# Group softmax: shorter programs, first tile loaded row by row, and stores that stand one row sooner

## The chip, the cores and the metric

The kernel runs on one core of a Trainium2 chip. The metric is device time in microseconds (us) of one execution. A *span* is the profiled execution; the time of the same run is 1.8 us longer. In the views DVE is VectorE, ACT is ScalarE and SP is SyncE; a q behind the name (ACTq, SPq) stands for the instruction queue of that engine, and L102 is a line of the kernel.

## The reference

```python
B, N, D, G = 4, 4096, 4352, 8                 # x: float32
x_g = x.reshape(B, N, G, D // G)              # 8 groups of 544 in a row
exp = np.exp(x_g - x_g.max(axis=-1, keepdims=True))
out = exp / exp.sum(axis=-1, keepdims=True)
```

There are 16,384 rows. 285 MB are read and 285 MB written. A tile is two rows on each of 128 partitions, so there are 64 tiles; "row n" below is row n of a partition, 0 to 127.

## The kernel before

SyncE issues the loads, into six tile buffers. VectorE takes each row's eight maxima and later scales the row. ScalarE does the exps with their sums, and issues the stores. A load waits until the store that used its buffer six tiles earlier is complete.

```python
def vector_max(n):
    s = n % S
    if s % R == 0:
        take(nc.vector, landed[s // R], 16)
        nc.vector.sem_inc(seen, 1)
    nc.vector.reduce_max(out=mx[:, s, :], in_=row(s), axis=X, negate=True).then_inc(max_done, 1)
...
def scalar_tile(j, *targets):                 # LAG = 2: tile j's exps, tile j-2's store
    take(nc.scalar, seen)
    for r in range(R):
        if r < len(targets):
            store((j - LAG + r) % NT, targets[r])
        scalar_exp(j * R + r)
...
for t in range(nt):                           # SyncE
    b = t % NT
    if t >= NT:
        nc.sync.wait_ge(stored[b], 16 * (t // NT))
    nc.sync.dma_start(out=bufs[b][:, :], in_=xt[t]).then_inc(landed[b], 16)
...
for j in range(LAG):                          # ScalarE
    scalar_tile(j)
with loop(nc.scalar) as u:                    # loop head placed at slot 0 of a fetch block
    for b in range(NT):
        scalar_tile(LAG + b, turn_out[u, b])
scalar_tile(nt - 2, ot[nt - 4])
scalar_tile(nt - 1, ot[nt - 3], ot[nt - 2])
store((nt - 1) % NT, ot[nt - 1])
...
def vector_rows(lo, hi):                      # VectorE
    for n in range(lo, hi):
        vector_max(n + 1)
        vector_scale(n)
```

## Time and profile before

| | before |
|---|---|
| time, median of 4 runs | 1329.49 us (1329.46 to 1329.67) |
| span of the profile | 1327.6 us |
| VectorE / ScalarE busy | 1206.9 us (91%) / 764.3 us (58%) |
| DMA | 570.48 MB, mean 430 GB/s |

The page's list of DMA issues gives the median time from issue to landing:

```profile
xt<-in_x_dram SPq DMA_DIRECT2D x64, 4352.0 KB, 29.2
out_dram<-xt ACTq DMA_DIRECT2D x64, 4352.0 KB, 51.2
```

A tile takes 20.57 us of DMA for its load and its store, so about 1.4 loads and 2.5 stores stand in the queues at any time.

### The profile page before, as it was taken

How to read it: one execution, taken by the hardware profiler on the slowest of the kernel's cores; microseconds unless marked ns; L12 is line 12 of the kernel's file. 1: busy time of each engine (PE TensorE's matmuls, PEld its weight loads, DVE VectorE, ACT ScalarE, POOL GpSimd, SP SyncE). 2: the span in 40 equal slices, each digit the busy share in tenths (PEclk: the TensorE clock that was granted, in tenths of full speed). 3: DMA queues.
4: the chain of work that ended last, by engine and by line, in shares of the span. 5: the costliest groups of instructions: out<-in, count | busy, mean ns of one | idle time of the engine just before them, and what ended most of it. 6: DMA issues, size and time to landing. Idle time of an engine off the chain costs nothing. (4 is left out here: it accounts for less than half of the span.)

```text
span 1327.6 us, 3432 instructions
## 1 busy us (share of the span) xinstructions
DVE 1206.9 (91%) x384; ACT 764.3 (58%) x2049; POOL 0.2 (0%) x4
## 2 busy tenths in 40 slices
DVE  5999999999999989899898898988989889898892
ACT  3565656565656655565565655655556555565551
POOL 0000000000000000000000000000000000000000
DMA  9999999999999999999999999999999999999997
GB/s 403 418 436 436 434 431 429 435 435 435 434 426 433 436 435 433 431 430 434 436 435 434 425 434 436 435 433 431 429 435 436 434 434 428 432 435 436 433 430 335
DMA packets 18438, 570.48 MB, mean 430 GB/s; under 512 B 2048, under 2 KB 2048, under 8 KB 2048
## 3 DMA queue, kind: packets, MB, share of 16 engines
q1 hardware_dynamic: 9216, 285.22, 49.8%
q10 hardware_dynamic: 9216, 285.22, 49.7%
q14 instruction: 6, 0.05, 0.0%
HBM read 285.21 MB, written 285.21 MB: 430 GB/s over the span
## 5 line engine op out<-in xcount | busy, mean ns | idle before, releaser
L90 ACT ACTIVATE xt<-xt,mx 128x544 f32<-128x544 f32 x1024 | 751.2, 734 | 534.9 <-ACTq L59 534.9
L70 DVE TENSOR_REDUCE mx<-xt 128x8 f32<-128x4352 f32 x128 | 599.0, 4681 | 76.7 <-DVEq L59 75.2
L78 DVE TENSOR_TENSOR xt<-xt,rs 128x4352 f32<-128x4352 f32 x128 | 600.6, 4692 | 18.8
L90 ACT ACTIVATION_READ_ACCUMULATOR xt<-xt,mx 128x1 f32 x1024 | 191.0, 187 | 0.0
L75 DVE RECIPROCAL rs<-sm 128x8 f32<-128x8 f32 x128 | 24.7, 193 | 2.9 <-DVEq L59 2.9
L122 ACT ACT_TABLE_LOAD x1 | 1.3, 1283 | 0.9 <-SPq L47 0.9
L158 POOL MEMSET const-bfloat16-1.0<- 128x1 bf16 x1 | 0.1, 102 | 0.0
L158 POOL MEMSET const-uint8-127<- 128x1 uint8 x1 | 0.1, 102 | 0.0
L158 POOL MEMSET const-float32-0.0<- 128x1 f32 x1 | 0.1, 100 | 0.2 <-issue 0.2
L158 POOL MEMSET const-float32-1.0<- 128x1 f32 x1 | 0.1, 99 | 0.0
## 6 DMA issues: line engine op xcount, KB each, us to landing
xt<-in_x_dram SPq DMA_DIRECT2D x64, 4352.0 KB, 29.2
out_dram<-xt ACTq DMA_DIRECT2D x64, 4352.0 KB, 51.2
```

Source lines behind the costliest of these rows:

```text
L70: nc.vector.reduce_max(out=mx[:, s, :], in_=row(s), axis=X, negate=True).then_inc(max_done, 1)
L75: nc.vector.reciprocal(out=rs[:, s, :], in_=sm[:, s, :]).then_inc(rec_done, 1)
L78: nc.vector.tensor_tensor(out=xr, in0=xr, in1=rs[:, s, :].unsqueeze(2).to_broadcast([P, G, Dg]), op=mybir.AluOpType.mult,).then_inc(scaled, 1)
L90: i = nc.scalar.activation(out=xr[:, g, :], in_=xr[:, g, :], func=Exp, bias=mx[:, s, g:g + 1], scale=1.0, accum_out=sm[:, s, g:g + 1],)
L122: nc.scalar.preload_act_table(Exp)
L158: nc = _bacc.Bacc("TRN2", target_bir_lowering=False, num_devices=1)
```

## The change

It makes the programs shorter, no longer places the loops at the head of a fetch block (a block is the piece in which an engine's program is fetched), and starts the compute sooner by loading the first tile row by row. It also moves the stores: tile t's store now stands behind the exp of row 2t+2, where before it stood behind that of row 2t+3. At the end, row 125 is scaled ahead of row 126's max, and the store of tile 62 stands ahead of the exp of row 126 instead of behind it.

```diff
-    with loop(nc.scalar) as u:                       # placed at a fetch block
-        for b in range(NT):
-            scalar_tile(LAG + b, turn_out[u, b])
...
+    for r in range(R):                               # first tile, row by row
+        nc.sync.dma_start(out=bufs[0][:, r * D:(r + 1) * D], in_=x0[:, r, :]).then_inc(
+            first[r - 1] if r else landed[0], 16)
...
+    scalar_exp(0)
+    with nc.scalar.Fori(0, turns) as u:
+        for t in range(NT):
+            for n in range(t * R + 1, t * R + R + 1):
+                scalar_exp(n)
+            store(t, turn_out[u, t])
+    for n in range(turns * S + 1, nr):
+        if n == (nt - 1) * R:
+            store(nt - 2, dram(of, nt - 2))
+        scalar_exp(n)
+        if n % R == 0 and n < (nt - 1) * R:
+            store(n // R - 1, dram(of, n // R - 1))
+    store(nt - 1, dram(of, nt - 1))
...
+    vector_rows(lead + turns * S, (nt - 1) * R - 1)
+    vector_scale((nt - 1) * R - 1)                   # row 125 scaled first
+    vector_max((nt - 1) * R)
+    vector_rows((nt - 1) * R, nr - 1)
+    vector_scale(nr - 1)
```

More of the change, by code (lines that the diff above doesn't have):

```diff
@@ L6 @@
 from concourse._compat import with_exitstack
-from concourse.ordered_engine_set import OrderedEngineSet
 @with_exitstack
@@ L22 @@
     S = R * NT
-    LAG = 2
     xf = x.flatten_outer_dims()
@@ L27 @@
     Dg = D // G
-    nt = N // (P * R)
-    turns = (nt - LAG) // NT
-    rest = LAG + turns * NT
-    assert rest == nt - 2
+    nr = N // P
+    nt = -(-nr // R)
+    last_rows = nr - (nt - 1) * R
+    turns = (nt - 2) // NT
     f32 = mybir.dt.float32
@@ L34, with dram @@
     Exp = mybir.ActivationFunctionType.Exp
-    xt = xf.rearrange("(t p r) d -> t p (r d)", p=P, r=R)
-    ot = of.rearrange("(t p r) d -> t p (r d)", p=P, r=R)
-    turn_out = of[:turns * S * P, :].rearrange("(u b p r) d -> u b p (r d)", b=NT, p=P, r=R)
+    def dram(af, t):
+        lo, r = P * R * t, R if t < nt - 1 else last_rows
+        return af[lo:lo + P * r, :].rearrange("(p r) d -> p (r d)", p=P)
+    turn_out = of[:turns * P * S, :].rearrange("(u b p r) d -> u b p (r d)", b=NT, p=P, r=R)
     landed = [tc.alloc_semaphore(f"landed{b}") for b in range(NT)]
+    first = [tc.alloc_semaphore(f"first{r}") for r in range(1, R)]
     stored = [tc.alloc_semaphore(f"stored{b}") for b in range(NT)]
-    seen = tc.alloc_semaphore("seen")
     max_done = tc.alloc_semaphore("max_done")
@@ L51, with tile_of @@
     rs = ctx.enter_context(nc.sbuf_tensor("rs", [P, S, G], f32))
-    def loop(engine):
-        return nc.Fori(
-            0, turns, engines=OrderedEngineSet([engine.engine]), head_slot={engine.engine: 0})
     def take(engine, sem, n=1):
         engine.sem_inc(sem, -n).wait_op(sem, n, "sem-ge")
+    def tile_of(t):
+        return bufs[t % NT][:, :(R if t < nt - 1 else last_rows) * D]
     def row(s):
@@ L68, in vector_max @@
             take(nc.vector, landed[s // R], 16)
-            nc.vector.sem_inc(seen, 1)
+        elif n < R:
+            take(nc.vector, first[n - 1], 16)
         nc.vector.reduce_max(out=mx[:, s, :], in_=row(s), axis=X, negate=True).then_inc(max_done, 1)
@@ L98, in scalar_exp, with store @@
         i.then_inc(exp_done, 1)
-    def store(b, target):
-        take(nc.scalar, scaled, R)
-        nc.scalar.dma_start(out=target, in_=bufs[b][:, :]).then_inc(stored[b], 16)
-    def scalar_tile(j, *targets):
-        take(nc.scalar, seen)
-        for r in range(R):
-            if r < len(targets):
-                store((j - LAG + r) % NT, targets[r])
-            scalar_exp(j * R + r)
-    for t in range(nt):
-        b = t % NT
+    def store(t, target):
+        take(nc.scalar, scaled, R if t < nt - 1 else last_rows)
+        nc.scalar.dma_start(out=target, in_=tile_of(t)).then_inc(stored[t % NT], 16)
+    x0 = xf[:P * R, :].rearrange("(p r) d -> p r d", r=R)
+    for r in range(R):
+        nc.sync.dma_start(out=bufs[0][:, r * D:(r + 1) * D], in_=x0[:, r, :]).then_inc(
+            first[r - 1] if r else landed[0], 16)
+    for t in range(1, nt):
         if t >= NT:
-            nc.sync.wait_ge(stored[b], 16 * (t // NT))
-        nc.sync.dma_start(out=bufs[b][:, :], in_=xt[t]).then_inc(landed[b], 16)
+            nc.sync.wait_ge(stored[t % NT], 16 * (t // NT))
+        nc.sync.dma_start(out=tile_of(t), in_=dram(xf, t)).then_inc(landed[t % NT], 16)
     for t in range(nt - NT, nt):
@@ L122 @@
     nc.scalar.preload_act_table(Exp)
-    for j in range(LAG):
-        scalar_tile(j)
-    with loop(nc.scalar) as u:
-        for b in range(NT):
-            scalar_tile(LAG + b, turn_out[u, b])
-    scalar_tile(nt - 2, ot[nt - 4])
-    scalar_tile(nt - 1, ot[nt - 3], ot[nt - 2])
-    store((nt - 1) % NT, ot[nt - 1])
+    scalar_exp(0)
[11 more added lines that the diff above has]
+    store(nt - 1, dram(of, nt - 1))
     def vector_rows(lo, hi):
@@ L136, in vector_rows @@
             vector_scale(n)
+    lead = R - 1
     vector_max(0)
-    vector_rows(0, LAG * R)
-    with loop(nc.vector):
-        vector_rows(LAG * R, LAG * R + S)
-    vector_rows(rest * R, nt * R - 1)
-    vector_scale(nt * R - 1)
+    vector_rows(0, lead)
+    with nc.vector.Fori(0, turns):
+        vector_rows(lead, lead + S)
+    vector_rows(lead + turns * S, (nt - 1) * R - 1)
[3 more added lines that the diff above has]
+    vector_scale(nr - 1)
 _INS = ['x']
```

## The prediction

> **What bounds the kernel now.** I read the page's slices first, then its groups, then the DMA queue's waits, then the timeline and the windows of the two edges.
>
> ```profile
> DMA  9999999999999999999999999999999999999997
> DMA packets 18438, 570.48 MB, mean 430 GB/s; under 512 B 2048, under 2 KB 2048, under 8 KB 2048
> q14 instruction: 6, 0.05, 0.0%
> L90 ACT ACTIVATE xt<-xt,mx 128x544 f32<-128x544 f32 x1024 | 751.2, 734 | 534.9 <-ACTq L59 534.9
> L70 DVE TENSOR_REDUCE mx<-xt 128x8 f32<-128x4352 f32 x128 | 599.0, 4681 | 76.7 <-DVEq L59 75.2
> L78 DVE TENSOR_TENSOR xt<-xt,rs 128x4352 f32<-128x4352 f32 x128 | 600.6, 4692 | 18.8
> ```
>
> The DMA engines are full in every slice but the last. A row costs VectorE 4.68 + 4.69 + 0.19 = 9.55 us, a tile of two rows 19.1 us; a tile costs ScalarE 2 x 5.97 us (eight activations; the timeline's first row runs 18.94 to 24.91). The trace's packet records give the transfers: a tile is 8 packets of 34,816 B on each of 16 DMA engines, 1.288 us each and 1.285 us from start to start, so 10.285 us for a load or a store alone. Load and store of a tile take 20.57 us of DMA against 19.1 of VectorE: DMA is the bound, VectorE has 7% to spare. Each transfer also leaves 16 packets of 4 B, one an engine, by which I can time each engine.
>
> Sixty-four tiles are 1024 packets an engine: 1024 x 1.285 = 1315.8 us, starting at 1.96. Most engines end at 1319.8 to 1320.4, which leaves about 2 us for slow packets at the start and at the first store. Three end later, at 1321.2, 1322.4 and 1325.55. The last one slips by 0.094 us in every tile (its 4-byte packet of the loads is 5.2 us behind the median by load 63): it alone sets the end.
>
> ```profile
> 1309.00:1319.00 10.00, 0.00 (x0) 0.00 (x0) 0.00 (x0) 1.00 1.01 435
> 1319.00:1322.00 3.00, 0.00 (x0) 0.00 (x0) 0.00 (x0) 1.00 0.22 93
> 1322.00:1325.60 3.60, 0.00 (x0) 0.00 (x0) 0.00 (x0) 1.00 0.05 19
> ```
>
> In these windows (the last two columns are DMA share and GB/s) all compute is over and one engine drains alone. So only two things can move the time: how long that last engine is busy, and whether it ever runs dry.
>
> **What the Trainium skill says.** (1) "DMA: Bandwidth & Descriptors", Queues, rings and completion order: a DMA engine goes round-robin between the queues that have work. The trace agrees: with loads and stores both queued a tile takes 20.57 us, alone 10.29. (2) The same page, Latency and other measured facts: engines 7 and 15 are usually slower, with a guessed cause. Here one engine is, by 0.094 us a tile; the records I have do not number it. (3) "Runtime: NRT & Kernel Launch", Instruction fetch mechanics: each sequencer fetches its program by its own DMA queue in blocks of 16 KiB (256 instructions), and a taken branch outside the window stalls for a fetch. The trace agrees on the queue and the stall, not on the size: its fetches are 8192 B, so 128 slots of 64 B. They lie at 47.8, 53.7, 58.3, 64.5, 118.1 and 1267.8 us. ScalarE branches to its loop at 46.0 and goes on at 49.5, 1.3 us after the first fetch.
>
> **The change part by part.**
>
> *Fewer fetches.* Each fetch takes one DMA engine 0.31 us and lengthens its next packet by 0.24 to 0.54 us, so the six cost about 4 us of DMA engine time. The fetch at 1267.83 starts where the 4-byte packet of the engine that ends at 1322.4 ends (1267.82 to 1267.83): the ones I can place are not on the last engine. Worth: 0 on the path.
>
> *The first tile by rows.* 34,816 B take 1.288 us and 8,192 B 0.309, so 17,408 B about 0.648 (estimate): no DMA time is added. Row 0 lands 8 x 0.645 = 5.16 us sooner, at 8.4 instead of 13.55. VectorE starts 0.58 later as before, at 9.0. DMA stays full from 1.96 either way, so by itself this is worth 0.
>
> *The first store comes much earlier.* Before:
>
> ```profile
> 49.86 5.48 ACTq L102 DMA_DIRECT2D out_dram<-xt  x1
> ```
>
> Stores lag two tiles, and the first issue is stuck for 5.48 us; it ends 1.37 us after the fetch at 53.66, and every later store takes 0.34 us, so I read it as a wait for that fetch. Its first packet starts at 56.67. After: max of row 0 ends 13.6, exp 13.8 to 19.7, second exp to 25.7; VectorE scales row 0 from 20.2 to 24.9, takes row 2's max to 29.5, scales row 1 to 34.5; exp of row 2 runs to 35.6. The store stands behind that exp and issues with its last activation, at 35.2, with no fetch near. Adding 0.34 + 1.33: first packet at 36.9.
>
> *What that does to the balance.* From the first store on, each engine moves one load packet for one store packet while both queues hold some. So the number of tiles landed and not yet stored, call it A, freezes at what was loaded before stores began. Before, loads had six tiles in by 71.9 and ran dry until 80.85 while stores went on: A = 6 - 1.49 = 4.51. It is still 4.51 at load 63 (landed at 1273.7 by the median engine, with 59.49 stores done). After: two tiles had landed plus one at 33.75, and 36.9 is 0.31 tile further, so **A = 3.31**. The load queue then keeps 2.7 tiles and never runs dry; store 1 (issue 54.5) just meets the end of store 0 (58.6), later ones gain 1.5 us a tile.
>
> *The tail.* When the last load lands, A tiles of stores remain.
>
> ```profile
> 1279.82 4.69 DVE L70 TENSOR_REDUCE mx<-xt 128x8 f32<-128x4352 f32 x1 [1.48 <-DVEq L59]
> 1284.76 4.69 DVE L78 TENSOR_TENSOR xt<-xt,rs 128x4352 f32<-128x4352 f32 x1
> 1300.62 4.69 DVE L78 TENSOR_TENSOR xt<-xt,rs 128x4352 f32<-128x4352 f32 x1
> 1305.42 0.34 ACTq L102 DMA_DIRECT2D out_dram<-xt  x1
> ```
>
> Before: it lands on the slow engine at 1279.11, the last store issues at 1305.42, 26.3 us later, first packet about 1307.1; that engine has other stores until 1315.27, so it never idles (8 us to spare). After: the last landing moves to 1325.55 - 3.31 x 10.285 = 1291.5. The order of the last tile also changes: row 125 is scaled ahead of row 126's max. From the landing: exp of 125 ends at 0.4, its scale 0.9 to 5.6, max 126 to 10.2, exp 126 to 16.3, exp 127 to 22.3, scale 127 to 27.5, issue 27.6. The queue holds 2.31 tiles beside the last one, 23.8 us, so it runs dry for some 5 us. The last store issues at 1319.1; load 0 at an empty start took 12.6 us from issue to landing (0.95 to 13.55): 1331.7. Add 2.0 us to the span's end and 1.9 from span to time, both as before: **1335.6**.
>
> **The rivals.** (a) The first store is stuck for 5.5 us after all, since it is the first DMA of that queue. For it: only that one issue was slow. Against: SyncE's first took 0.38 us, and the fetch ends 1.37 us before. A would be 3.31 + 5.5/10.285 = 3.84, the queue lasts 29.2 us beside the last store, first packet of which is needed at 29.2: nothing lost, 1329.5. (b) Fetches do load the last engine, and the tail does not bite: four or five fewer, 0.7 us each, 1326. Against: the placed one is elsewhere, and the slip is even over the run. (c) VectorE becomes the bound by a later start: it has 7% to spare and starts 5 us sooner, so no. (d) A store queue that runs dry early (a fetch on ScalarE near slot 128 of its program): loads gain, A rises by up to 0.25, 1333.
>
> **Range and chances.** I give the tail about 0.7, (d) partly mixed into it, (a) 0.2, (b) 0.1. I shade the point to 1335.0. The range 1328.0 to 1338.0 takes in (a) and (d) and leaves 2.4 us for a longer tail. Two per cent is 26.6 us, which nothing here reaches: faster 0.01, same 0.98, slower 0.01.
>
> **What would show it.** First store issue near 35 us and short; at the last load's landing about 3.3 tiles of stores left rather than 4.5; DMA share falling well below full for several us between 1310 and 1320, then full again for the last store; the last issue near 1319; one or two fetches during the run. I am wrong if DMA stays full to 1320 (then A was higher, or the last tile quicker), or if the late engine is no longer late.

## The result, and the profile after

The changed kernel took **1332.38 us** (median of 4, 1332.17 to 1332.48), against 1329.49 before: 2.9 us longer. The ratio is 1.0021, with a 95% interval of 1.0004 to 1.0039. By the 2% rule that is the same. A ratio here is the mean time of one kernel's runs over that of the other's runs of the same rounds, so it is not quite the ratio of the medians.

The page after, in the rows that answer to those of before:

```profile
DMA  9999999999999999999999999999999999999996
q14 instruction: 4, 0.03, 0.0%
L70 DVE TENSOR_REDUCE mx<-xt 128x8 f32<-128x4352 f32 x128 | 599.1, 4681 | 85.8 <-DVEq L55 85.8
out_dram<-xt ACTq DMA_DIRECT2D x64, 4352.0 KB, 39.0
xt<-in_x_dram SPq DMA_DIRECT2D x63, 4352.0 KB, 54.2
```

The work of an instruction is unchanged, and two fetches of six are gone. What changed is the last two rows. Loads now stand 54.2 us in their queue and stores 39.0, where before it was 29.2 and 51.2. The queue has turned from stores to loads, and when the loads are over there is less left to do.

The timeline after, first store and last tile (start, duration, what):

```profile
34.54 0.40 ACTq L102 DMA_DIRECT2D out_dram<-xt  x1
...
1291.12 4.69 DVE L78 TENSOR_TENSOR xt<-xt,rs 128x4352 f32<-128x4352 f32 x1
1295.73 9.27 DVE L70 TENSOR_REDUCE mx<-xt 128x8 f32<-128x4352 f32 x2
1306.99 4.69 DVE L78 TENSOR_TENSOR xt<-xt,rs 128x4352 f32<-128x4352 f32 x1
1312.84 4.69 DVE L78 TENSOR_TENSOR xt<-xt,rs 128x4352 f32<-128x4352 f32 x1
1317.63 0.34 ACTq L102 DMA_DIRECT2D out_dram<-xt  x1
```

The first store issues at 34.5 and is not held up; before, it issued at 49.9 and was held up for 5.48 us. The last load lands at 1290.4 (before 1279.1), and the last store issues at 1317.6 (before 1305.4). The windows at the end of the changed kernel show what DMA did in between (the stretch, its length, busy time of VectorE, ScalarE and GpSimd, PEclk, which is 1.00 throughout, and then DMA share and GB/s):

```profile
1301.00:1311.00 10.00, 8.22 (x3) 10.00 (x29) 0.00 (x0) 1.00 0.82 355
1311.00:1316.00 5.00, 4.04 (x3) 1.34 (x4) 0.00 (x0) 1.00 0.05 21
1316.00:1321.00 5.00, 1.53 (x1) 0.00 (x0) 0.00 (x0) 1.00 0.52 223
1321.00:1326.00 5.00, 0.00 (x0) 0.00 (x0) 0.00 (x0) 1.00 1.04 446
1326.00:1331.00 5.00, 0.00 (x0) 0.00 (x0) 0.00 (x0) 1.00 0.52 223
```

Between 1311 and 1316 DMA stands almost still while VectorE and ScalarE finish the last tile, and then it runs full for the last store alone. The trace also keeps a record of every DMA packet, with its queue, start, duration and size, but not the number of its DMA engine. By these records, the median DMA engine ends the store of tile 62 at 1309.9 and the slowest at 1314.9; the last store's first packets start at 1318.5. The slowest engine was dry (without work) for 3.6 us, the median one for 8.6.

### The profile page after: what moved, and what is told of

Read it like the earlier page. It is cut to its first block, busy times and chain, and to the rows that moved or that the text cites. A ratio compares the mean times of both kernels' runs of the same rounds, so it can differ in the third digit from the quotient of the medians.

```text
span 1330.7 us, 3304 instructions
## 1 busy us (share of the span) xinstructions
DVE 1208.2 (91%) x384; ACT 764.2 (57%) x2049; POOL 0.2 (0%) x4
## 6 DMA issues: line engine op xcount, KB each, us to landing
xt<-in_x_dram SPq DMA_DIRECT2D x63, 4352.0 KB, 54.2
xt<-in_x_dram SPq DMA_DIRECT2D x2, 2176.0 KB, 10.1
```

## The experiments

The theory in one line: the number of tiles landed but not yet stored, A, freezes when stores begin. At the last landing, A tiles of stores remain, of which all but the last must cover the compute of the last tile. I read A from each trace at the landing of tile 62 (loads landed less stores done, by the median DMA engine, a store in progress counted by its share of the time between two landings): 4.51 before, 3.375 after. A is not quite frozen everywhere: with the first tile by rows in the kernel before it goes from 4.63 at tile 40 to 4.50, and without placed loops there from 4.57 at tile 10 to 4.30.

How long the slowest engine is dry can be worked out from A: the time from the last landing to the first packet of the last store, less (A - 1) x 10.285 us of other stores. In the changed kernel the first is 27.3 us to the issue and 0.85 from there to the packets (1317.63 to 1318.48), so 28.1 - 24.4 = 3.7 us dry, and 3.6 was measured. Four buffers (A = 2.75) give 10.1, measured 10.1; the end order of before (26.2 us to the issue) gives 2.6, measured 2.5; A = 3.875 leaves nothing dry, and none was seen.

Ten kernels were made, and one of them was run twice. They were run at other times. Times are medians. The kernel before, in the same calls, took 1329.58, 1329.46 and 1329.60 us. The changed kernel was not run again in them; with five buffers, where A is the same, it took 1332.26 us there. Against the kernel before, every one of them is the same by the 2% rule; differences of 1 to 9 us from the changed kernel are read here only where the ranges do not overlap, unless the text says so.

| kernel | A | expected | us (range) |
|---|---|---|---|
| changed | 3.375 | | 1332.38 (1332.17 to 1332.48) |
| changed, first tile whole | 3.875 | 1329.3 | 1329.23 (1328.87 to 1329.31) |
| changed, stores a tile later | 4.50 | 1329.3 | 1327.62 (1327.53 to 1329.12) |
| the same again | | 1327.6 or 1329.3 | 1327.75 (1327.54 to 1332.17) |
| changed, end order of before | 3.375 | 1331.4 | 1331.37 (1330.97 to 1331.52) |
| changed, four buffers | 2.75 | 1339.4 | 1340.97 (1339.68 to 1341.73) |
| changed, five buffers | 3.375 | 1332.4 | 1332.26 (1332.22 to 1332.56) |
| changed, last tile stored by rows | 3.375 | 1328.7 | 1328.79 (1328.50 to 1328.90) |
| changed, loops at fetch blocks | 3.59 | 1332.4 | 1331.99 (1329.22 to 1339.19) |
| before, loops not at fetch blocks | 4.30 | 1329.5 | 1329.47 (1328.73 to 1332.96) |
| before, first tile by rows | 4.50 | 1329.5 | 1329.80 (1327.90 to 1329.98) |
| before, a load on 15 engines | | 1326 to 1331 | 1337.34 (1335.81 to 1339.44) |

One correction to texts: where they give the first packet of the first store (36.15 in the changed kernel, 56.67 before), I had taken the first lengthened *load* packets for it. By queue, its first packets start at 39.6 and 60.1.

### First tile loaded whole

```diff
-    for r in range(R):
-        nc.sync.dma_start(out=bufs[0][:, r * D:(r + 1) * D], in_=x0[:, r, :]).then_inc(
-            first[r - 1] if r else landed[0], 16)
+    nc.sync.dma_start(out=tile_of(0), in_=dram(xf, 0)).then_inc(landed[0], 16)
```

> The changed kernel with its first tile loaded in one piece, as before. Theory (the balance A, tiles landed and not yet stored, is frozen by the time of the first store's first packet; the changed kernel has A = 3.38 and its DMA runs dry before the last store): the first max starts at 14.1 instead of 8.8 us, the first store's packets start some 5.3 us later, at about 41.4, so A rises by 0.5 to about 3.9; the queue then lasts 29.7 us beside the last store against some 28.9 until that store's first packet; DMA does not run dry, and the time is 1329.3 (1328.9 to 1330.2). Rival 1 (the loss is the order of the last tile, or the fetch blocks, or the loop): unchanged at 1332.4. Rival 2 (loading by rows is a gain, as intended, of 5 us of latency): 1335 to 1337.

It took 1329.23 us. The first store issues at 39.78 instead of 34.54 and A rises by 0.5. The windows of this kernel:

```profile
1311.00:1316.00 5.00, 1.23 (x1) 0.00 (x0) 0.00 (x0) 1.00 0.80 341
1316.00:1321.00 5.00, 0.00 (x0) 0.00 (x0) 0.00 (x0) 1.00 0.90 390
```

Where the changed kernel showed 0.05, this one shows 0.80. The slowest engine ends tile 62 at 1314.8, after the last store's first packets start (1313.2), so it is never dry. Making the first row arrive *later* takes off 3 us. Loading by rows, taken out here, does no harm in the kernel before:

### The kernel before, with its first tile by rows

```diff
+        if t == 0:
+            x0 = xf[:P * R, :].rearrange("(p r) d -> p r d", r=R)
+            for r in range(R):
+                nc.sync.dma_start(out=bufs[0][:, r * D:(r + 1) * D], in_=x0[:, r, :]).then_inc(
+                    first if r else landed[0], 16)
+            continue
```

> The kernel before with its first tile loaded row by row: that part of the change alone. Theory: the first max starts at 8.8 instead of 14.1 us, but the first store still stands two tiles back and waits for the fetch at the loop, so its packets start at about 51, all six loads get ahead, A stays 4.5 to 4.75, DMA stays full, 1329.5 (1328.5 to 1330.0). Rival (loading by rows costs the 3 us by itself, wherever it is done): 1332.4.

It took 1329.80 us: the theory's figure, not the rival's. A is 4.50 here, so there are stores enough to cover the end. What costs 3 us in one kernel costs nothing in the other, because of what else stands in the queue.

### Stores a tile later

```diff
-    scalar_exp(0)
+    for n in range(R + 1):
+        scalar_exp(n)
...
-            for n in range(t * R + 1, t * R + R + 1):
+            for n in range(t * R + R + 1, t * R + 2 * R + 1):
...
+    store(turns * NT, dram(of, turns * NT))
-    for n in range(turns * S + 1, nr):
+    for n in range(turns * S + R + 1, nr):
```

> The changed kernel with each store inside the loop issued one tile (two rows of exp) later, the last four stores where they were. Theory: first store's packets at about 55, loads get five to six tiles ahead, A about 4.75; DMA stays full to its end, which the slowest DMA engine sets as in the kernel before: 1329.3 (1328.9 to 1329.8), last store issued about 15 us earlier than in the changed kernel (1303). Rival (stores that come later can only delay the loads that wait for them): 1332.4 or slower.

It took 1327.62 us, faster than the changed kernel and 1.7 us under what I expected; the second time 1327.75:

> The kernel with stores a tile later once more, as it beat both kernels by 1.9 us in four of five runs, which the theory (1329.3) does not give. If that is a property of the kernel, 1327.6 again with the slowest DMA engine ending near 1323.9; if it was chance of that chip, 1329.3.

Its windows:

```profile
1311.00:1316.00 5.00, 0.00 (x0) 0.00 (x0) 0.00 (x0) 1.00 0.98 425
1316.00:1321.00 5.00, 0.00 (x0) 0.00 (x0) 0.00 (x0) 1.00 0.84 362
```

DMA stays full, as the theory says. The remaining 1.7 us are where the slowest engine ends: at 1323.9 in both profiles, against 1325.55 in the kernel before, with three more engines near 1323. Why it is less late there I cannot say. Two of its ten runs took 1329.1 and 1332.2, and both intervals (0.9974 to 1.0002, 0.9982 to 1.0007) include 1. It beats both kernels by its medians, but is not proved faster than the kernel before.

### The order of the last tile

```diff
-        if n == (nt - 1) * R:
-            store(nt - 2, dram(of, nt - 2))
         scalar_exp(n)
-        if n % R == 0 and n < (nt - 1) * R:
+        if n % R == 0:
             store(n // R - 1, dram(of, n // R - 1))
...
-    vector_rows(lead + turns * S, (nt - 1) * R - 1)
-    vector_scale((nt - 1) * R - 1)
-    vector_max((nt - 1) * R)
-    vector_rows((nt - 1) * R, nr - 1)
+    vector_rows(lead + turns * S, nr - 1)
```

> The changed kernel with the order of before in the last tile alone: max of row 126 ahead of the scale of row 125 (and the store of tile 62 behind exp 126). Theory: the last store issues about 1.0 us sooner after the last landing (26.3 instead of 27.3), A and the landing stay, so 1331.4 (1331.0 to 1331.8). Rival 1 (this order is the cause of the whole loss): 1329.5. Rival 2 (DMA sets the end, the compute tail is hidden): 1332.4.

It took 1331.37 us, 1.0 less than the changed kernel. The last store issues 26.2 us after the last landing instead of 27.3 (1289.9 to 1316.1). So this part of the change (both orders together, VectorE's and that of tile 62's store) costs 1.0 of the 2.9 us. That it costs nothing where DMA does not run dry was not tried by itself; the kernels with the first tile whole and with later stores keep the new order, and their medians are no higher than that of the kernel before.

### Four and five buffers

```diff
-    NT = 6
+    NT = 4        # and NT = 5
```

> The changed kernel with four tile buffers instead of six: a dose of the suspected cause in the other direction. Theory: loads run dry at about 51 us, A falls to about 2.7; the last landing comes 0.7 tile = 7 us later than 1290.4, DMA is dry for about 12 us before the last store instead of about 5 on the slow engine, 1339.4 (1336 to 1343). Rival (A does not matter, a DMA engine that always has some work loses nothing by fewer buffers): within 1 us of 1332.4.

> The changed kernel with five tile buffers. Theory: what counts is A and not the number of buffers; with five, load 5 is asked for when store 0 is complete, at 60 us, and load 4 lands at 72, so loads do not run dry and A stays 3.38: 1332.4 (1331.9 to 1332.9), where four buffers (A 2.67) took 1341. Rival (every buffer taken away costs a share of those 8.6 us): 1336 to 1337.

With four buffers the time is 1340.97 us, A is 2.75, and the windows show the gap grown:

```profile
1311.00:1316.00 5.00, 3.21 (x3) 5.00 (x15) 0.00 (x0) 1.00 0.54 230
1316.00:1321.00 5.00, 4.04 (x3) 3.57 (x10) 0.00 (x0) 1.00 0.00 0
1321.00:1326.00 5.00, 3.76 (x1) 0.00 (x0) 0.00 (x0) 1.00 0.26 111
```

The slowest engine is dry for 10.1 us (1315.65 to 1325.7). With five buffers A is 3.375, as with six, and the time 1332.26 us. So it is A that counts, not the number of buffers. In the changed kernel the sixth buffer buys nothing.

### The last tile stored by rows

```diff
-    store(nt - 1, dram(of, nt - 1))
+    for r in range(R):
+        take(nc.scalar, scaled)
+        nc.scalar.dma_start(out=o_last[:, r, :], in_=bufs[(nt - 1) % NT][:, r * D:(r + 1) * D]).then_inc(
+            stored[(nt - 1) % NT] if r == R - 1 else last_row, 16)
```

> The changed kernel with the last tile stored in two pieces of one row each. Theory: the first piece (5.15 us of every DMA engine) is issued at about 1311.8, before the slowest engine has run dry at 1314.9, the second at 1317.6; that engine is then busy to 1325.3 and the time is 1328.7 (1328.0 to 1329.5): the loss is gone without touching A. Rival (the loss is not the dry time at the end): within 1 us of 1332.4.

It took 1328.79 us with A left at 3.375. Its last issues and windows:

```profile
1311.32 0.34 ACTq L137 DMA_DIRECT2D out_dram<-xt  x1
1317.18 0.34 ACTq L137 DMA_DIRECT2D out_dram<-xt  x1
...
1311.00:1316.00 5.00, 4.04 (x3) 0.89 (x4) 0.00 (x0) 1.00 0.80 338
```

The gap of 0.05 is 0.80 again. The first piece is issued at 1311.3, before the slowest engine ends tile 62 (1314.5); that engine then works on to 1324.8 without a pause. Closing the dry time takes off 3.6 us with A unchanged. This and the first experiment close the same gap from its two sides.

### The fetch blocks: taken from the kernel before, given to the changed one

```diff
-            0, turns, engines=OrderedEngineSet([engine.engine]), head_slot={engine.engine: 0})
+            0, turns, engines=OrderedEngineSet([engine.engine]))
```

(the kernel before; the changed kernel got the opposite edit on both its loops)

> The kernel before with its two loops no longer placed at the head of a fetch block: the fetch part of the change, nearly alone. Theory (what a fetch costs does not lie on the slowest DMA engine; the first store merely stops being stuck for 5.5 us, and A is 4.5 to 4.75 either way, so DMA never runs dry): 1329.5 (1328.5 to 1330.0). Rival (fetches do load the slowest DMA engine; the kernel with later stores, which has two fetches fewer than the kernel before, ended 2 us sooner than the theory said): 1327 to 1328.

> The changed kernel with both loops placed at the head of a fetch block, as before: the fetch part of the change undone. Theory: the extra fetches now come at 14 to 25 us, while the first exps are still ahead, so the first store, at 34.5, finds none under way and is not stuck; A stays 3.38 and the time 1332.4 (1331.5 to 1333.0). Rival (the blocks decide, because a first store that meets a fetch is stuck for 5 us, which raises A to 3.9): 1329.5. Rival 2 (more fetches cost DMA time on the path, 0.7 us each): 1334 to 1335.

Neither median moves: 1329.47 and 1331.99 us. But both kernels scatter, by 4 and by 10 us, where the changed kernel's own runs lie within 0.3. In the profiled run of the changed kernel with placed loops (1337.2 us) two DMA engines were 10 us behind the median at the last landing, where the changed kernel has one that is 4.9 behind. With placed loops A came out at 3.59, where I had expected 3.38. So the comparison says little on half a per cent, and what sets the scatter is open.

These runs do say more on what held up the first store. I had expected it not to be held up once the loops are not placed, and it was, for 4.28 us: a miss. Its issue in the kernel before without placed loops, then in the kernel before with the first tile by rows, then in the changed kernel with placed loops:

```profile
46.42 4.28 ACTq L102 DMA_DIRECT2D out_dram<-xt  x1
```

```profile
44.66 5.49 ACTq L105 DMA_DIRECT2D out_dram<-xt  x1
```

```profile
36.62 0.40 ACTq L103 DMA_DIRECT2D out_dram<-xt  x1
```

In the first two a fetch ends at 49.34 and 48.77, and the issue ends at 50.70 and 50.15, 1.36 and 1.38 us later; in the kernel before it was 1.37. In the third, the fetches come at 19 to 31 us and none is under way. So the hold-up does not come with the first DMA of a queue as such; it goes with a fetch, and ends at the same distance from it each time. Not every fetch does this: in the changed kernel a store issued at 110.88 us, during a fetch from 110.61 to 110.92, took 0.34 us. The records do not say for which engine a fetch is, so that only ScalarE's own fetches hold up its issues is likely, but not shown.

### A load spread over 15 DMA engines

```diff
+        if t == nt - 1:
+            nc.sync.dma_start(out=bufs[b][:120, :], in_=xt[t][:120, :]).then_inc(landed[b], 16)
+            nc.sync.dma_start(out=bufs[b][120:, :], in_=xt[t][120:, :]).then_inc(rest8, 16)
+            continue
```

> The kernel before with the last tile's load in two pieces: partitions 0 to 119, which the Trainium skill (DMA: Bandwidth & Descriptors, Why a DMA increments its semaphore by 16 and not by 1) says go to the 15 lowest-numbered engines, and 120 to 127, to the 8 lowest. Engine 15 is thereby spared 8 packets, 10.3 us. Theory (one DMA engine, the last one by number, is late and alone sets the end of the kernel before): it ends before the others, and the next late one sets the end, at 1322.4 or a packet later, so 1326.3 to 1327.6. If the late engine is one of 0 to 7, it gets one packet more: 1330.8. If it is one of 8 to 14, or if the late engine does not set the end: 1329.5.

It took 1337.34 us, a miss. DMA was slow while the last tile's load ran, as two windows of this kernel show, ahead of it and during it:

```profile
1230.00:1253.00 23.00, 21.22 (x8) 11.92 (x32) 0.00 (x0) 1.00 1.00 433
1253.00:1280.00 27.00, 23.34 (x9) 16.37 (x45) 0.00 (x0) 1.00 1.01 334
```

The share is the same and the rate a quarter lower: each packet takes longer, load packets 1.7 to 2.4 us on average in stretches of 3 us instead of 1.29. The records do show that one engine was spared (one fewer 4-byte packet, 1031 in the load queue where 1024 + 15 + 8 - 16 are due), and that the latest engine still ended last, 6.0 us behind the median at the end. The spared engine shows as well: some engine had stored tile 58 at 1258.8, 9.0 us ahead of the median, while the load of tile 62 landed on the late one only at 1260.5. So the late engine is not the spared one. Which it is, and why, stays open. The cause that the Trainium skill guesses at for slow engines, which the prediction mentions, is by the same row of that page one of DMAs issued by GpSimd; here SyncE and ScalarE issue all of them.

## Why the prediction was right, and where it was off

It said 1335.0 us, in a range of 1328.0 to 1338.0, and the same within 2%; measured 1332.38.

- **The bound, and that compute time does not matter**: right. Both engines' busy times are as before, and the time follows when DMA is busy.
- **Fewer fetches are worth nothing**: right as far as the medians of the two placed and unplaced kernels go. I expected one or two fetches and there were four. A fetch matters in one indirect way: by its timing, it held up the first store of the kernel before.
- **The first store comes much earlier**: right, 34.54 for 35.2, and short. The end of its issue moved from 55.34 to 34.94, by 20.4 us: 5.2 from loading by rows (the experiment moved it from 34.54 to 39.78), 5.1 from the hold-up that is gone (5.48 to 0.40), and the other 10.1 by its new place in the program, since a row takes 9.55.
- **The balance freezes at A = 3.31**: right in kind, and 3.375 by the trace. The step behind it was wrong twice. The first packet came at 39.6 and not 36.9, since it starts 4.7 us after the issue ends and not 1.3 (the reading of 56.67 as the first packet before was wrong, as said above). In that time load packets took up to 2.1 us instead of 1.29, so fewer loads got in (3.39 tiles at 39.6). That the two nearly cancel is luck.
- **DMA runs dry before the last store**: right, 3.6 us on the slowest engine where I said some 5. Four edits that close the gap, narrow it or widen it (first tile whole, last tile by rows, end order, four buffers) moved the time as they should.
- **The sizes of the tail**: this is where the 3.2 us between my sum, 1335.6, and the measurement lie. The last landing was put at 1291.5 and came at 1290.4 (1.1 us). The issue after it was put at 27.6 and came at 27.3 (0.3). The last store from issue to landing was put at 12.6, from the first load of the program, and took 11.3, 1317.63 to 1328.96 (1.3). The two ends, put at 2.0 and 1.9, were 1.7 and 1.8 (0.4). The point was shaded to 1335.0, so it missed by 2.6. The late engine's lag, given as 5.2 us by load 63, is 5.4 by the prediction's own landings (1279.11 and 1273.7).
- **The rivals**: the hold-up of the first store did not recur (0.40 us); fetches showed no effect on the medians, as far as their scatter lets one see; VectorE did not become the bound; the store queue did not run dry early.

What the change was meant to win was hidden anyway: DMA was full from 2.0 us on, whenever the first row was ready. What it lost came from the first store being so early, of which loading by rows is one part and the store's new place another, with the order of the last tile adding 1.0 us.

## What to carry to other kernels

Where loads and stores share DMA engines that are full all the time, as here, an earlier first store saved nothing; it fixed how far loads run ahead, and so how many stores are left to cover the compute of the last tile. Before making a start faster, work out what will be in the queue at the end. If the end is bare, store the last tile in pieces as they are ready (here 3.6 us), or let stores stand later (4.6 to 4.8 us by the medians, though not in every run).

## What the Trainium skill lacked or had wrong

- "Runtime: NRT & Kernel Launch", Instruction fetch mechanics, gives blocks of 16 KiB (256 instructions); every fetch packet in these traces is 8192 B, and some stand alone (118.1 and 1267.8 us in the kernel before). Whether the size is wrong or a setting, no run shows. All fetches stand in one queue of the trace, q14, so whether each engine has its own is not seen. The section tells of a stall at a taken branch, and lacks that a DMA issue can be held up around a fetch: 5.48, 4.28, 5.49 and 5.49 us in four kernels (the fourth is the one with a load on 15 engines), each ending 1.36 to 1.38 us after the fetch; 0.34 to 0.40 us for every other store.
- "DMA: Bandwidth & Descriptors", Latency and other measured facts, gives about 0.6 us to the first byte. The last store of the changed kernel, on idle DMA, started packets 0.5 us after its issue ended (1317.97 to 1318.48) and 0.85 after it began, which is near; the first store's, behind a full load queue, took 4.7 us from the end of the issue in both kernels (34.94 to 39.59; 55.34 to 60.08). I found no rate there for a load on 15 engines: here 334 GB/s, loads and stores together, around the time it ran, against 433 just before.
- I found no page with the consequence shown here: with both queues full, the number of tiles landed and not stored stays nearly constant (4.51 before and 3.375 after, from tile 10 to tile 62; in some of the other kernels it drifted, by up to 0.28).
